# Dilated attention in a two-block fp32 program: operands split at the projection, a copy in eighths order, and softmax from head 0 up

## The chip, the cores and the metric

The program runs on one core of one Trainium2 chip. The metric is the device time of one execution in microseconds (us), the median of a few runs. Matrix products run on TensorE (PE in the rows, its weight loads PEld), elementwise work on VectorE (DVE) and ScalarE (ACT), a little on GpSimd (POOL), and SyncE (SP) issues nearly all DMAs.

## The reference

Two blocks follow each other on x of 1024 tokens by 1024 channels, in fp32. The first is a hybrid layer: an RMS norm, one projection, a gated delta rule ("GDN", 4 heads of 128), dilated attention (8 heads of 64), an output projection and a gated feed-forward. The second (spatial gating and a 31-tap convolution, then a feed-forward) is not touched by the diff. The part that matters:

```python
DIL_PATTERNS = ((128, 1), (512, 4), (2048, 16))
def dilated_attention(q, k, v):           # each (window, dilation): t, t-d, ..., t-window
    qf = q.transpose(0, 2, 1, 3) * (Dh ** -0.5)
    ...
    for window, dil in DIL_PATTERNS:
        num, den, m = band_attention(stride(qf), stride(kf), stride(vf), window // dil)
    ...
    m_all = jnp.maximum(jnp.maximum(ms[0], ms[1]), ms[2])
    wts = [jnp.exp(mi - m_all) for mi in ms]
    num_tot = wts[0] * nums[0] + wts[1] * nums[1] + wts[2] * nums[2]
    den_tot = wts[0] * dens[0] + wts[1] * dens[1] + wts[2] * dens[2]
    out = num_tot / den_tot
```

One maximum m_all per query over all three patterns is needed before the exponentials.

## The kernel before

**Precision.** A product of two fp32 operands is made of matmuls in a faster fp32 form (`fp32r`): each operand is split into a high part, rounded to that form, and a low part, the rest. For attention scores the splits are stacked over the partitions of one tile, so that two matmuls give a whole score block: one over 128 partitions (64 rows high part, 64 rows high or low part, tiles `KA`, `QA`) and one over 97 (64 rows, and rows 64 and 96, which add minus the maximum in the second pass; tiles `KB`, `QB`).

**Order.** The code is written as tasks (generators). A planner, run when the program is built, holds an assumed clock for each engine; `cost` adds the assumed time of each operation (`mm` for matmuls, `tp` for transposes, `act`, `tt`, `stt`, `dma`), and `run` always takes the task that, by these clocks and the tasks' priorities, can go next. What is emitted is a fixed order on every engine. Changing an assumed cost can so change the order anywhere. Tiles come from two arenas in SBUF, R (`arR`, fp32r operands) and F (`arF`, fp32); a task that asks for `room` waits until something is given back.

**The dilated part.** `proj1` computes queries and keys feature-major (`ps_dil`, 8 tiles of 128 rows by two halves of 512), ScalarE evacuates each, and they go to DRAM (`qd`, `kd`); values (`ps_dv`) follow. `dil` then makes two passes over the heads.

- The scan (`dil_scan`) takes a slot of 4 x 1024 words per head out of three, loads and splits keys and queries (`dil_split`: per operand two DMAs of 64x1024 into a staging tile, then ScalarE and VectorE), and computes 16 blocks of scores with *queries as the stationary operand* (`ps_S<-arR`, 32 matmuls a head). Eight blocks are 128 consecutive queries against their own and the previous block of keys ("pattern 0"). Eight are the queries r, r+8, r+16, ... ("eighths") against the 256 keys congruent to r modulo 4, which covers the other two patterns through a mask. VectorE adds the mask and takes each row's maximum in one operation (`djunk`, L1246). `dil_max` merges the maxima of four heads and writes them to DRAM (`mf`).
- The second pass (`dil_pv`) computes the scores again with *keys as the stationary operand* (`ps_T<-arR`, 32 matmuls a head), adds the mask on VectorE (tile `band`), takes the exponential on ScalarE, and multiplies by the values (`ps_O<-arF`, 48 matmuls a head). Heads come as 7, 6, 5, ..., 0; slots of heads 7 and 6 are kept from the scan, the others are loaded and split a second time (14 loads and splits in all are so made: 8 in the scan, 6 in the second pass). `dil_fin` divides and writes the operand of the output projection `ps_out`.

For the eighths blocks both operands are read with a step of 8 words (32 bytes): the stationary one is `slice(r, S, 8)`, the moving one comes from `eights`. The second pass waits for all maxima and for a reload of the mask (`band`), whose place was used by another half of it until the last maximum. When head 2 is done, its slot is given back and the weights of the output projection are fetched (`WH`, `weights(2)`).

The scan has the lowest priority of what PE can do at that time (7, against 2 for GDN), so that its matmuls fill the gaps in GDN's chains of small dependent matmuls (`ps_T<-arF`, `ps_pU`, `ps_G`, `ps_u`, `ps_o`).

Of the kernel before, what the change touches and what calls it, by code (L numbers as in the profile page):

```python
# [17 lines left out]
P = 128  # L18
# [73 lines left out]
class Weaver:  # L92
# [11 lines left out]
    STEP, SCP, KEEP1, KEEP0, WH = 2, 7, 2, 0, 2  # L104
# [154 lines left out]
class Prog(Weaver):  # L259
# [28 lines left out]
    def tp(self, out, in_):  # L288
        k = in_.shape[0]
        self.cost("PE", 107.0)  # L290
        self.nc.tensor.transpose(out, in_, self.ident[:k, :k])

    def tpacc(self, out, in_, start):

        self.cost("PE", 107.0)
# [307 lines left out]
    def proj1(self):  # L603
# [5 lines left out]
        self.qd, self.kd = d("qd", 512, S), d("kd", 512, S)  # L609
        self.ab = self.cp.tile([P, NT, 8], F32, name="ab")  # L610
        self.ssq = self.cp.tile([P, 8, NT], F32, name="ssq")
        raw, hl, st = self.fring(2, 2080), self.fring(3, 4160, "R"), self.fring(2, 520)
# [463 lines left out]
    def dil(self):  # L1076
# [5 lines left out]
        stg, heads = Ring([]), Ring([])  # L1082
        yield "SP", after(self.gmem)
        yield from self.more(stg, 2, S)
        mb = yield from self.room(2 * P)
        M = v3(mb.ap, P)
        scans, kept, maxs = [[], []], {}, [Ev(), Ev()]

        def head():
            b = yield from self.room(4 * S, arena=self.R)  # L1090
            heads.bufs.append(b)
            s = Slot(b.ap)
            s.buf = b
            self.spawn(self.dil_aug(s, heads), prio=4, eng="ACT")
# [12 lines left out]
        def scan():  # L1107
            for n, h in enumerate(range(8)):
                yield "SP", after(self.qkev[h // 4])
                s = yield from heads.get("SP")  # L1110
                keep = h in (7, 6)[:int(self.KEEP1)] or h in (3, 2)[:int(self.KEEP0)]
                if keep:
                    kept[h] = s
                scans[h // 4].append(self.spawn(self.dil_scan(h, s, None if keep else heads, stg, M), prio=int(self.SCP), eng="SP"))
# [6 lines left out]
            self.dma(self.band, self.a["c_band"][:, 768:1536], 393216)  # L1121
            self.turned.set(self.ready())

        self.turned = Ev()
# [31 lines left out]
        def allv():  # L1156
            yield "SP", after(self.vev)
            for pr in (3, 2, 1, 0):
                yield from loadv(pr)
# [3 lines left out]
        fins, last, loads = [], [], []  # L1163
# [952 lines left out]
```

## Time and profile before

| | us |
|---|---|
| median of 3 runs (lowest to highest) | 2617.27 (2617.18 to 2620.52) |
| the profiled execution's own time | 2619.11 |
| its span in the trace | 2617.3 |
| busy in the span: PE, DVE, ACT, POOL | 2540.3, 1370.7, 807.9, 121.1 |
| DMA bytes moved in the span | 170.80 MB |
| mean granted TensorE clock | 0.987 |

The profiled execution is 1.84 us above the median. PE has work for 97% of the span, so time is lost only in the gaps that its stages leave, or gained where its own instructions get shorter or fewer. The stages, on the span's time: projections to about 222 us, GDN with the dilated projections and the scan to about 636, the second pass to about 769, output projection and feed-forward to about 1600, and from there the second block to the end.

### The profile page before, as it was taken

The page shows a single profiled execution, that of the slowest core. Times are in us where ns is not written, and L with a number is a line of the kernel's source. Part 1 is how long each engine was busy: PE and PEld are TensorE (multiplying, and loading weights), DVE is VectorE, ACT ScalarE, POOL GpSimd, SP SyncE. Part 2 cuts the span into 40 slices and gives each one's busy share as a digit, 9 for nine tenths or more (in the row PEclk, how much of TensorE's full clock was granted, in tenths as well). Part 3 has the DMA queues.
Part 4 walks back from the last instruction along what each step waited for, and adds up shares of the span by engine and source line. Part 5 has one row for each costly group of instructions (what it writes and reads, how often), then busy time and mean ns, then how long its engine had stood idle before and what let it go on. Part 6 is the DMA issues. An engine that isn't in the chain of part 4 may idle for free.

```text
span 2617.3 us, 31361 instructions
## 1 busy us (share of the span) xinstructions
PE 2540.3 (97%) x13001; PEld 2180.4 (83%) x13001; DVE 1370.7 (52%) x1868; ACT 807.9 (31%) x1306; POOL 121.1 (5%) x245
## 2 busy tenths in 40 slices
PE   7999999988989999999999999989999999999998
PEld 6888999988978888888888888877788888888887
DVE  5441343454654555555555567969554444444444
ACT  5322443453541422222222235253232121212122
POOL 1010000000000000000000001050000000000000
PEclk9999999998989999999999999999999999999999
DMA  5232222232441111111111113102211111111111
GB/s 189 71 104 85 84 67 62 80 80 69 106 130 57 41 49 49 49 50 50 49 50 49 50 66 101 61 9 90 71 41 57 41 57 41 57 41 57 41 49 65
DMA packets 175164, 170.80 MB, mean 65 GB/s; under 512 B 25985, under 2 KB 148254, under 8 KB 175022
## 3 DMA queue, kind: packets, MB, share of 16 engines
q1 hardware_dynamic: 175022, 168.80, 21.2%
q8 instruction: 102, 1.67, 0.3%
q14 instruction: 40, 0.33, 0.0%
HBM read 145.50 MB, written 23.23 MB: 64 GB/s over the span
## 4 chain that ended last, share of the span: by engine, by line
PE 61%; issue 28%; DVE 4%; ACT 3%; DMA 2%; POOL 2%; SPq 0%; POOLq 0%; ACTq 0%; DVEq 0%
PE ps_up L281 18%; PE ps_dn L281 9%; PE ps_in L281 5%; PE ps_out L281 5%; PE ps_vg L281 3%; PE ps_dil L281 3%; PE ps_T L281 2%; ACT arF L311 2%; PE ps_S L281 2%; PE ps_z L281 2%; PE ps_O L281 2%; PE ps_dv L281 2%; DVE arF L327 2%; PE ps_pU L281 1%; PE ps_G L281 1%
## 5 line engine op out<-in xcount | busy, mean ns | idle before, releaser
L281 PE MATMUL ps_up<-arR 128*128 128x512 f32 x3648 | 831.5, 389 | 0.0
L281 PEld LDWEIGHTS ps_up<-arR 128*128 128x128 f32 x3648 | 684.5, 188 | 142.1
L315 DVE TENSOR_TENSOR arR<-arF,arR 128x1024 fp32r<-128x1024 f32 (+3 forms) x283 | 347.6, 1236 | 610.0 <-ACT arR L311 609.5
L281 PE MATMUL ps_dn<-arR 128*128 128x512 f32 x2592 | 591.8, 389 | 0.0
L311 ACT ACTIVATE arR<-arF 128x1024 fp32r<-128x1024 f32 (+3 forms) x297 | 311.2, 1071 | 852.3 <-PE ps_dn L281 394.3
L281 PEld LDWEIGHTS ps_dn<-arR 128*128 128x128 f32 x2592 | 486.4, 188 | 101.0
L315 DVE TENSOR_TENSOR arF<-arF,ps_dn 128x512 f32<-128x512 f32 x416 | 279.6, 684 | 183.2 <-PE ps_dn L281 183.2
L327 DVE SCALAR_TENSOR_TENSOR arF<-arF,pcol 128x1024 f32<-128x1024 f32 (+1 forms) x276 | 311.4, 1149 | 22.5 <-ACT arF L311 17.5
L311 ACT ACTIVATE arF<-arF 128x1024 f32<-128x1024 f32 (+3 forms) x158 | 134.8, 860 | 272.5 <-DVE arF L315 138.5
L281 PE MATMUL ps_out<-arR 128*128 128x512 f32 x768 | 182.2, 398 | 2.7 <-DVE arR L315 2.7
L281 PEld LDWEIGHTS ps_out<-arR 128*128 128x128 f32 x768 | 146.7, 192 | 34.4 <-DVE arR L315 3.7
L311 ACT ACTIVATE arF<-ps_up 128x512 f32<-128x512 f32 x152 | 89.5, 589 | 187.0 <-PE ps_up L281 187.0
L281 PE MATMUL ps_in<-arR 128*128 128x512 f32 x576 | 137.7, 399 | 0.0
L281 PEld LDWEIGHTS ps_in<-arR 128*128 128x128 f32 x576 | 109.4, 192 | 23.9
L315 DVE TENSOR_TENSOR arF<-arF 128x1024 f32<-128x1024 f32 (+4 forms) x91 | 89.1, 979 | 28.8 <-ACT arF L311 14.8
L281 PE MATMUL ps_dil<-arR 128*128 128x512 f32 x384 | 97.4, 403 | 0.0
L281 PE MATMUL ps_vg<-arR 128*128 128x512 f32 x384 | 88.3, 390 | 0.0
L281 PEld LDWEIGHTS ps_vg<-arR 128*128 128x128 f32 x384 | 71.8, 188 | 14.8
L281 PEld LDWEIGHTS ps_dil<-arR 128*128 128x128 f32 x384 | 71.7, 192 | 14.2
L281 PE MATMUL ps_O<-arF 128*128 128x128 f32 (+2 forms) x384 | 69.9, 328 | 12.2 <-ACT arF L311 6.8
L315 DVE TENSOR_TENSOR arF<-ps_G,csq 128x512 f32<-128x512 f32 x48 | 33.1, 690 | 90.8 <-PE ps_G L281 90.8
L315 DVE TENSOR_TENSOR arF<-arF,ps_out 128x512 f32<-128x512 f32 x64 | 43.5, 683 | 62.1 <-PE ps_out L281 62.1
(185 smaller groups left out, 2037.2 us busy)
## 6 DMA issues: line engine op xcount, KB each, us to landing
arF<-in_w_ff_dram SPq DMA_DIRECT2D x64, 512.0 KB
arF<-in_w_up_dram SPq DMA_DIRECT2D x44, 512.0 KB
arF<-in_w_in_dram SPq DMA_DIRECT2D x12, 1024.0 KB
arF<-in_w_down_dram SPq DMA_DIRECT2D x22, 512.0 KB
arF<-in_x_dram SPq DMA_DIRECT2D x16, 512.0 KB
arF<-in_w_out_dram SPq DMA_DIRECT2D x16, 512.0 KB
arF<-in_w_in_dram SPq DMA_DIRECT2D x16, 512.0 KB
arF<-kd SPq DMA_DIRECT2D x28, 256.0 KB
```

Of the source, the lines that this page charges most:

```text
L281: self.nc.tensor.matmul(out, lhsT, rhs, start=start, stop=stop, **kw)
L311: self.nc.scalar.activation(out, in_, func, **kw)
L315: self.nc.vector.tensor_tensor(out, a, b, op)
L327: self.nc.vector.scalar_tensor_tensor(out, a, s, b, op0, op1)
```

## The change

1. Queries and keys are split where they are evacuated from PSUM: ScalarE writes the high part, VectorE subtracts it from PSUM, and four tensors go to DRAM (`qh`, `ql`, `kh`, `kl`) with 32 stores of 256 KB in the place of 16. The staging slots there are twice as large.
2. `dil_split` and its staging ring are gone. `dil_fetch` brings three DMAs of 64x1024 words per operand, the stacked operand ready to use: six for each head in each pass. No slot is kept from the scan to the second pass, so 16 head loads (96 DMAs) are made where 14 (56 DMAs) were.
3. `dil_turn` makes a copy of the operand that is to be stationary, ordered by eighths (two ScalarE operations of 1024 columns a head and pass, which read with a step of 32 bytes). Stationary operands of eighths blocks are then consecutive columns. The moving operand is still read through `eights`.
4. The three slots of 4 x 1024 words become two `mov` slots (moving operand) and four `sta` slots (stationary operand, the eighths copy) of 2 x 1024 words. A head needs one `mov` and two `sta`, in either pass.
5. The mask of the second pass has a buffer of its own (`bb`, 768 words of F), loaded once at the start of `dil`.
6. The second pass takes heads 1, 0, 3, 2, 5, 4, 7, 6, each waiting for the maxima of its own group of four heads. `WH` is 7: weights are fetched from the last pair on.
7. The planner's assumed costs of matmuls and transposes change, with an assumed 240 ns for a matmul whose stationary operand is strided.

```diff
     def mm(self, out, lhsT, rhs, start, stop, loose=False):
         n, m = cols(rhs), cols(lhsT)
+        load = 112.0 if m > 64 else 56.0
         if rhs.dtype == F32:
-            c = max(1.667 * n, 213.0 if m > 64 else 107.0)
+            c = max(1.667 * n + 5.0, 2.0 * load)
         elif rhs.dtype == F32R:
-            c = max(0.417 * n, 107.0 if m > 64 else 56.0)
+            far = lhsT.ap[-1][0] > 1
+            c = max(0.417 * n + 13.3, 240.0 if far else load)
...
-                            self.act(s.ap[:, :H], ps, AF.Copy, scale=(0.125, 1.0)[part])
-                            self.dma((self.qd, self.kd)[part][m * P:(m + 1) * P, hf * H:(hf + 1) * H], s.ap[:, :H])
+                            hi, lo = (s.ap[:, x * H:(x + 1) * H].bitcast(F32R) for x in range(2))
+                            self.act(hi, ps, AF.Copy, scale=(0.125, 1.0)[part])
+                            if part:
+                                self.tt(lo, ps, hi.bitcast(F32), ALU.subtract)
+                            else:
+                                self.stt(lo, ps, 0.125, hi.bitcast(F32), ALU.mult, ALU.subtract)
+                            for x, dst in enumerate(self.qk[part]):
+                                self.dma(dst[m * P:(m + 1) * P, hf * H:(hf + 1) * H], s.ap[:, x * H:(x + 1) * H], 262144)
...
         mb = yield from self.room(2 * P)
         M = v3(mb.ap, P)
+        bb = yield from self.room(768)
+        self.dma(bb.ap, self.a["c_band"][:, 768:1536], 393216)
...
         def memory():
-            heads.bufs = []
-            yield from head()
+            yield from unit(mov)
+            yield from unit(sta)
             yield from self.opiece(1, 0)
-            for _ in range(2):
-                yield from head()
+            for r in (sta, mov, sta, sta):
+                yield from unit(r)
...
+        def load():
+            yield "SP", after(got)
+            for h in (1, 0, 3, 2, 5, 4, 7, 6):
+                box[h] = []
+                for r in (sta, sta, mov):
+                    box[h].append((yield from r.get("SP")))
+                kn, kr, q = box[h]
+                self.dil_fetch(1, h, kn)
+                e = self.spawn(self.dil_turn(kn, lambda kr=kr: kr), prio=4, eng="ACT")
+                self.dil_fetch(0, h, q)
+                self.spawn(self.dil_rows(h, q, after(e, maxs[h // 4]), here[h]), prio=4, eng="SP")
...
+    def dil_fetch(self, x, h, s):
         r = slice(h * 64, h * 64 + 64)
+        hi, lo = (d[r, :] for d in self.qk[x])
+        A, B = (s.ap[:, j * S:(j + 1) * S].bitcast(F32R) for j in range(2))
+        for o, i in ((A[0:64], hi), (A[64:128], (lo, hi)[x]), (B[0:64], (hi, lo)[x])):
+            self.dma(o, i, 262144)
+
+    def dil_turn(self, a, other):
+        yield "ACT", lambda: 0.0 if other() else -1.0
+        b = other()
+        turn = lambda t: t.rearrange("p (m r) -> p r m", r=8)
+        for o, n in ((0, P), (S, 64)):
+            self.act(v3(b.ap[:n, o:o + S], P), turn(a.ap[:n, o:o + S].bitcast(F32)))
...
+        yield "PE", after(turn)
+        self.put(sta, q)
+        q = other[0]
+        self.hold = True
         for g in range(4):
             yield "PE", after(*evs[-2:-1])
             ps = self.psum("S8")
             for x in range(2):
-                scores(ps[:, x * 256:x * 256 + 256], slice(g + 4 * x, S, 8), lambda t: self.eights(t, g))
+                r = g + 4 * x
+                scores(ps[:, x * 256:x * 256 + 256], q.ap, slice(r * P, (r + 1) * P), lambda t: self.eights(t, g))
```

What it moves, as the order of the built programs shows it. First PE in the midst of GDN, where the chain matmuls (`<-arF`) of one chunk stand between scan matmuls (`ps_S<-arR`) and projection matmuls (`ps_dil`). Before:

```order
L281 MATMUL ps_S<-arR 128x128 x2
L281 MATMUL ps_S<-arR 128x256 x2
L281 MATMUL ps_G<-arF 128x128 x4
L281 MATMUL ps_u<-arF 128x128 x8
L281 MATMUL ps_T<-arF 128x128 x4
L281 MATMUL ps_pU<-arF 128x128 x4
L281 MATMUL ps_S<-arF 128x128 x4
L281 MATMUL ps_o<-arF 128x128 x8
L281 MATMUL ps_G<-arF 128x128 x4
L281 MATMUL ps_S<-arR 128x256 x8
L281 MATMUL ps_dil<-arR 128x512 x6
```

The same place of the chunk's chain with the change:

```order
L283 MATMUL ps_dil<-arR 128x512 x24
L298 MATMUL ps_T<-csq,arF 128x128 x4
L283 MATMUL ps_dil<-arR 128x512 x6
L283 MATMUL ps_u<-arF 128x128 x8
L283 MATMUL ps_dil<-arR 128x512 x6
L283 MATMUL ps_S<-arF 128x128 x4
L283 MATMUL ps_o<-arF 128x128 x8
L298 MATMUL ps_pU<-csq,arF 128x128 x4
L283 MATMUL ps_G<-arF 128x128 x4
L283 MATMUL ps_dil<-arR 128x512 x6
L283 MATMUL ps_T<-arF 128x128 x4
L283 MATMUL ps_pU<-arF 128x128 x4
```

There is no scan matmul left here: only `ps_dil` (and later `ps_dv`) stands between the chains. The second place is PE at the end of GDN. Before, with the last chains:

```order
L281 MATMUL ps_S<-arR 128x256 x8
L281 MATMUL ps_G<-arF 128x128 x4
L281 MATMUL ps_S_4714<-arR 128x256 x4
L281 MATMUL ps_T<-arF 128x128 x4
L281 MATMUL ps_pU<-arF 128x128 x4
L291 MATMUL ps_ot<-csq,arF 128x128 x4
L281 MATMUL ps_S_4744<-arR 128x256 x4
L281 MATMUL ps_S_4749<-arR 128x256 x4
L281 MATMUL ps_G<-arF 128x128 x4
L281 MATMUL ps_S_4764<-arR 128x256 x4
L281 MATMUL ps_pU<-arF 128x128 x4
L291 MATMUL ps_mt<-csq,mt 16x128
```

With the change, the same chains and what follows them:

```order
L283 MATMUL ps_T<-arF 128x128 x4
L283 MATMUL ps_pU<-arF 128x128 x4
L283 MATMUL ps_G<-arF 128x128 x4
L293 MATMUL ps_ot<-csq,arF 128x128 x4
L283 MATMUL ps_T<-arF 128x128 x4
L283 MATMUL ps_pU<-arF 128x128 x4
L283 MATMUL ps_G<-arF 128x128 x4
L283 MATMUL ps_pU<-arF 128x128 x4
L283 MATMUL ps_S_4275<-arR 128x256 x4
L283 MATMUL ps_S_4282<-arR 128x256 x4
L283 MATMUL ps_S<-arR 128x128 x2
L283 MATMUL ps_S<-arR 128x256 x2
```

The chains stand alone, and the scan begins behind them: apart from 16 matmuls of head 0, which stand earlier, 240 of its 256 matmuls come in one piece here, with only the last `ps_w`, `ps_u`, `ps_o` and `ps_ot` of GDN among them. The third place is SP at the start of the second pass (`vd` are values, `mf` maxima, `kd` and `qd` the operands). Before:

```order
L339 DMA arF<-zd 128x512
L339 DMA arF<-vd 128x8x64 x4
L339 DMA arR<-mf_102 1x1024
L339 DMA arR<-mf_103 1x1024
L339 DMA arR<-mf_102 1x1024
L339 DMA arR<-mf_103 1x1024
L339 DMA arF<-kd 64x1024 x4
L339 DMA band<-in_c_band_dram 128x768
L339 DMA arF<-in_x_dram 128x1024 x2
L339 DMA arF<-qd 64x1024 x2
```

With the change (`md` are the row maxima of one head on their way to the merge):

```order
L341 DMA arR<-kh 64x1024 x2
L341 DMA arR<-kl 64x1024
L341 DMA arR<-qh 64x1024
L341 DMA arR<-ql 64x1024
L341 DMA arR<-qh 64x1024
L341 DMA arF<-md 8x128
L341 DMA arF<-md 8x8x16
L341 DMA md<-mtt 16x128
L341 DMA arR<-mf_104 1x1024
L341 DMA arR<-mf_105 1x1024
```

The first heads' operands are asked for ahead of the last maxima, values have been loaded well before, the mask's load is gone from here, and a head has six loads of 64x1024 in the place of four.

## Rows read from the trace of the kernel before

**Rows 1.** The page, part 1: busy time of each engine.

```profile
PE 2540.3 (97%) x13001; PEld 2180.4 (83%) x13001; DVE 1370.7 (52%) x1868; ACT 807.9 (31%) x1306; POOL 121.1 (5%) x245
```

**Rows 2.** Windows by stage: length, then busy us of each engine (instructions), clock, DMA.

```profile
core 0: us, PE busy (x) PEld busy (x) DVE busy (x) ACT busy (x) POOL busy (x), PEclk, DMA share, GB/s
222.00:636.00 414.00, 395.90 (x2869) 374.10 (x2867) 172.72 (x489) 179.21 (x358) 13.30 (x25) 0.99 0.24 70
636.00:650.00 14.00, 6.13 (x28) 5.29 (x28) 5.39 (x11) 2.59 (x5) 1.41 (x3) 0.76 1.06 266
650.00:769.00 119.00, 109.28 (x617) 104.13 (x618) 74.15 (x110) 66.13 (x97) 2.10 (x4) 0.94 0.46 117
769.00:800.00 31.00, 28.99 (x112) 23.23 (x112) 15.62 (x19) 4.99 (x5) 0.00 (x0) 0.88 0.39 119
1600.00:1860.00 260.00, 244.31 (x1316) 208.40 (x1316) 213.97 (x237) 98.57 (x235) 41.84 (x49) 0.97 0.20 63
```

**Rows 3.** The chain of waits around the start of the second pass: start, us.

```profile
637.88 4.56 DMA arF<-vd
643.12 5.33 DMA band<-in_c_band_dram
650.04 2.05 PE ps_O L281 x8
```

**Rows 4.** Timeline of PE in the second pass, runs of like matmuls: start, us.

```profile
660.09 1.30 PE L281 MATMUL ps_T<-arR 128*128 128x256 f32 x4
661.22 1.04 PE L281 MATMUL ps_O<-arF 128*128 128x256 f32 x4
661.91 2.27 PE L281 MATMUL ps_T<-arR 128*128 128x256 f32 x8
664.00 2.25 PE L281 MATMUL ps_O<-arF 128*128 128x256 f32 x11
```

**Rows 5.** Groups by form, 222 to 800 us: count, busy us, mean ns, idle before.

```profile
L281 PE MATMUL ps_dv<-arR 128*128 128x256 f32 x384 | 49.1, 283 | 0.0
L1246 DVE CUSTOM_DVE_ANT_0 djunk<-ps_S,band 128x256 f32<-128x256 f32 x120 | 45.4, 419 | 17.7 <-PE ps_S L281 17.0
L315 DVE TENSOR_TENSOR arR<-arF,arR 64x1024 fp32r<-64x1024 f32 x28 | 34.1, 1217 | 26.1 <-ACT arR L311 25.7
L311 ACT ACTIVATE arR<-arF 64x1024 fp32r<-64x1024 f32 x14 | 14.6, 1044 | 0.0
L315 DVE TENSOR_TENSOR arF<-ps_T,band 128x512 f32<-128x512 f32 x56 | 37.2, 687 | 22.3 <-PE ps_T L281 20.0 <-ACT arF L311 1.3 <-DMA band<-in_c_band_dram 0.9
```

**Rows 6.** Timeline of DVE in the scan, two row maxima in close order.

```profile
588.83 0.42 DVE L1246 CUSTOM_DVE_ANT_0 djunk<-ps_S,band 128x256 f32<-128x256 f32 x1
589.18 0.42 DVE L1246 CUSTOM_DVE_ANT_0 djunk<-ps_S,band 128x256 f32<-128x256 f32 x1
```

**Rows 7.** Timeline of SP: one issue of four loads of 64x1024.

```profile
640.68 2.40 SPq L339 DMA_DIRECT2D arF<-kd  x4
```

**Rows 8.** DMA view, 640 to 656 us, 40 slices of 0.4 us.

```profile
GB/s 229 216 218 191 104 164 287 287 318 215 266 215 246 236 241 233 202 200 366 397 461 369 440 369 461 389 317 246 215 236 174 21 10 20 0 0 0 0 0 0
```

**Rows 9.** Timeline of ACT: 512 columns read in order, and with a step (`dil_fin`).

```profile
649.27 1.83 ACT L311 ACTIVATE arF<-arF 128x512 f32<-128x512 f32 x3 [2.86 <-DVE arF L315]
697.74 2.08 ACT L311 ACTIVATE arR<-arF 128x512 fp32r<-128x512 f32 x2
```

**Rows 10.** The chain of waits inside the second pass: start, us.

```profile
716.23 3.78 DMA rd<-den
721.81 5.72 DMA arF<-qd
727.61 2.00 ACT arR L311 x2
```

**Rows 11.** PE's waits, 1600 to 1860 us: total, times, longest.

```profile
PE ps_ct L281 <- DVE arF L327: 7.8, 2, 5.6
PE ps_c L281 <- ACT arF L311: 6.4, 1, 6.4
```

More of the change, by code (lines that the diff above doesn't have):

```diff
@@ L103 @@
     ISSUE, N1P, SSL, CLL = 475.0, 2, 6000.0, 1500.0
[L104 removed]
+    STEP, SCP, WH = 2, 7, 7
     KP0, KP1, KP2, KP3 = 0, 0, 0, 3
@@ L1109, in scan @@
                 yield "SP", after(self.qkev[h // 4])
[L1110 to L1114, printed above, removed]
+                k = yield from mov.get("SP")
+                q = yield from sta.get("SP")
+                scans[h // 4].append(self.spawn(self.dil_scan(h, k, q, mov, sta, M, got if h == 7 else None), prio=int(self.SCP), eng="SP"))
                 if n % 4 == 3:
@@ L1157, in allv @@
             yield "SP", after(self.vev)
-            for pr in (3, 2, 1, 0):
+            for pr in range(4):
                 yield from loadv(pr)
@@ L1162, in dil @@
         self.spawn(allv(), prio=6, eng="SP")
-        fins, last, loads = [], [], []
-        for pr in (3, 2, 1, 0):
+        box, here = {}, [Ev() for _ in range(8)]
+        def load():
[10 more added lines that the diff above has]
+                self.hold = True
+                yield "SP"
+        self.spawn(load(), prio=4, eng="SP")
+        fins, last = [], []
+        for pr in range(4):
             den, ob = [], {}
@@ L1167, in dil @@
                 h = 2 * pr + hh
-                yield "SP", after(*maxs, self.vev)
-                box = [kept.get(h)]
-                e = self.spawn(self.dil_load(h, box, heads, stg), prio=3, eng="SP")
-                loads.append(e)
-                last = [self.spawn(self.dil_pv(pr, hh, box, e, V, vr, ptr, stage, ob, heads), prio=5, eng="PE")]
+                yield "SP", after(self.vev)
+                last = [self.spawn(self.dil_pv(pr, hh, box, here[h], bb.ap, V, vr, ptr, stage, ob, mov, sta), prio=5, eng="PE")]
                 den += last
@@ L1176, in dil @@
             fins.append(self.spawn(self.dil_fin(pr, ob, den, stage, recr), prio=4, eng="SP"))
-        yield "SP", after(*loads)
-        yield from self.drain(stg, 2)
         yield "SP", after(*last)
-        for r, n in ((heads, 2), (ptr, int(self.PTR))):
+        bb.give()
+        for r, n in ((sta, 2), (mov, 1), (ptr, int(self.PTR))):
             yield from self.drain(r, n)
@@ new lines, in dil_rows, with dil_scan, room @@
+    def dil_rows(self, h, q, cond, done):
+        yield "SP", cond
+        for r, d in zip((64, 96), self.mf):
+            self.dma(q.ap[r:r + 1, S:2 * S].bitcast(F32), d[h:h + 1, :])
+        done.set(self.ready())
+    def dil_scan(self, h, k, q, mov, sta, M, got):
+        nc = self.nc
+        self.dil_fetch(0, h, q)
+        self.dil_fetch(1, h, k)
+        landed = self.ready()
+        KA, KB = (k.ap[:, j * S:(j + 1) * S] for j in range(2))
+        other = []
+        def room():
+            other.append((yield from sta.get("ACT")))
+            if got:
+                got.set(self.ready())
+        turn = self.spawn(self.dil_turn(q, lambda: other and other[0]), prio=4, eng="ACT", t=landed)
+        self.spawn(room(), prio=4, eng="ACT", t=0.0)
@@ L1269, in dil_scan @@
                 self.hold = True
-        if heads is not None:
-            self.put(heads, s)
+        self.put(sta, q)
+        self.put(mov, k)
         yield "PE", after(*evs)
@@ L1312, in dil_max, with dil_pv, back @@
         done.set(self.ready())
-    def dil_load(self, h, box, heads, stg):
-        if not box[0]:
-            yield from self.dil_split(h, box, stg, heads)
-        QB = box[0].ap[:, 3 * S:]
-        for r, d in zip((64, 96), self.mf):
-            self.dma(QB[r:r + 1].bitcast(F32), d[h:h + 1, :])
-    def dil_pv(self, pr, hh, box, e, V, vr, ptr, stage, ob, heads):
-        h = 2 * pr + hh
-        yield "PE", after(e, self.turned)
-        hs = box[0]
-        KA, KB, QA, QB = (hs.ap[:, j * S:(j + 1) * S] for j in range(4))
+    def dil_pv(self, pr, hh, box, e, mk, V, vr, ptr, stage, ob, mov, sta):
+        h = 2 * pr + hh
+        yield "PE", after(e)
+        kn, kr, q = box.pop(h)
+        QA, QB = (q.ap[:, j * S:(j + 1) * S] for j in range(2))
+        def back(ring, s):
+            if h == int(self.WH):
+                s.buf.give()
+            else:
+                self.put(ring, s)
         loaded = lambda pat: lambda: V[pr, pat][2].t if (pr, pat) in V else -1.0
```

93 lines of the change are left out of this document (34 added, 59 removed).

## The prediction, on record before the change was run

> **What bounds the kernel now.** I read the busy times first: PE works for 97% of the span and DVE for 52% [rows 1]. So the time is PE's own work plus its gaps, and the windows by stage say where the gaps are [rows 2]. From 222 to 636 us (GDN, dilated projections, scan) PE is busy for 395.9 of 414 us: 18 us of gaps. From 636 to 650 it is busy for 6.1 of 14 us, at a granted clock of 0.76, while the DMA share is 1.06. The second pass, 650 to 769, holds 109.3 us of PE work in 119 us. Then 2 of 31 us are idle, and in the start of the second block (1600 to 1860) 15.7 of 260. DVE and ACT are far from full in all of these but the last, where DVE has 214 of 260 us.
>
> The chain of waits explains the gap at 636: values are loaded until 642.4, then the mask of the second pass from 643.1 to 648.5, and only at 650.0 does the first product with values start [rows 3]. That is a start-up stall of about 14 us with 6 us of work in it.
>
> The price of a strided stationary operand comes from PE's timeline [rows 4]. Four eighths matmuls take 661.22 - 660.09 = 1.13 us, eight take 664.00 - 661.91 = 2.09 us. The difference is 0.24 us a matmul, and each run pays about 0.17 us more at its ends. The 256-column matmuls of the value projection, both operands in order, are 384 in 49.1 us, 0.128 us each [rows 5]. So 128 eighths matmuls of the second pass carry up to 128 x (0.24 - 0.128) = 14.3 us that the stride costs, and as much again in the scan.
>
> **The change, part by part.** *Split at the projection.* 16 more DVE operations of 128x512 out of PSUM, about 0.69 us each by the mask addition of that shape [rows 5], are 11 us. They fall between 222 and 440, within the stretch where DVE is busy for 173 of 414 us [rows 2]. Cost 0 while `ps_dil` is filler; if each held a PSUM buffer for its 0.69 us in PE's way, 11 us. I take 0. The 16 more stores (16 x 0.6 us of SP, by the issue rate in [rows 7]) lie in the same stretch, where nothing is queued behind them that PE soon needs.
>
> *Splits removed.* 28 DVE operations of 1.22 us (34 us) go [rows 5], with the ScalarE operations ahead of them. They are off the path except where a head's load is late in the second pass: `qd` lands after 5.72 us and two ScalarE operations take 2.00 us more [rows 10]. In their place a head has six loads (1.57 MB) for four.
>
> *The copy by eighths.* The trace has no matmul with a stationary operand in order and a moving one with a step. Lower bound 0.128 us, as both in order; upper bound 0.24, as both strided, for then the change of the weights' order buys nothing. A weight load has 128 columns and the moving pass 256, so both may be near 0.24 or only the load. I take 0.20, nearer to the strided row, since the moving operand keeps its stride. That saves 0.04 us a matmul and most of the 0.17 us at a run's ends. Per head of the second pass PE now has 109.3 / 8 = 13.7 us; with four runs a head, it loses 16 x 0.04 + 4 x 0.17 = 1.3 us and has about 12.3 us. The copy costs ScalarE two operations of 1024 columns: 1.04 us each if the step costs nothing [rows 5], and 2 x 1.04 us each by the stepped read of 512 columns, which takes 1.04 us where 512 in order take 0.61 [rows 9]. I take the upper end, 4.1 us a head, as that read too has a step. ScalarE has 66 of 119 us in the second pass; 8 x 4.1 = 33 us more, less 6 heads' splits, leave it under 90.
>
> *The scan moved behind GDN.* The order shows it: with the change nothing but `ps_dil` and `ps_dv` fills GDN's gaps, its last chains stand alone, and 240 of the 256 scan matmuls come after. Scan work inside 222 to 636 was 128 x 0.128 + 128 x 0.24 + 32 x 0.17 for the runs' ends = 52 us; 2 us of it (16 matmuls) stay ahead. So without the scan the stretch has 395.9 - 52 + 2 = 346 us of PE work, of which about 5 us (`ps_w`, `ps_u`, `ps_o`) stand inside the later scan: 341. Its 18 us of gaps do not all go, since the last chains have no filler: I keep 14. It then ends at 222 + 341 + 14 = 577 us.
>
> The scan alone, per head: PE 16 x 0.128 + 16 x 0.20 = 5.3 us; DVE 16 maxima at a start-to-start of 0.35 us [rows 6] = 5.5 us; SP six issues at 0.60 us [rows 7] and three small ones, about 4.5 us; 1.57 MB at the 250 GB/s that the view shows while many loads are under way [rows 8], 6.3 us; ScalarE's copy up to 4.1 us. No resource needs more than 6.3 us, but a head holds one of two `mov` slots from its first load to its last matmul: 3.6 us of issues, some 5 us until the last has landed, half the copy (2 us) beyond pattern 0's 2.7 us, then 2.6 us: 14 us, for two heads at a time 7 us each. Two heads are loaded ahead: 2 x 5.5 + 5.5 x 7 = 50 us. Lower bound 7.5 x 5.5 = 41 us (DVE alone), upper bound below. The second pass then begins at 627, its first value product at about 629, where it was 650.0.
>
> *The second pass.* 8 x 12.3 = 98 us of PE work, plus the 9.7 us of gaps that the old one has within 119, is 108 us. What is late next there is the slot again: two heads may be under way, and the third one's six loads start when the first gives its slots back, then the copy (up to 4.1 us) and the two rows of maxima, some 14 us for the 12.3 us that the head between needs. That would add up to 2 us a head; against it, the loads no longer wait for splits. I keep the 9.7 us and let the range go 12 us up. The pass ends at 737, where it was 769: 32 us earlier. Start-up stall, shorter matmuls and the copies' cost are all within this number.
>
> *After it.* Weights of the output projection are asked for about one head before the end, where they had more than two heads; the gap of 2 us there may grow by 2. The planner's new costs also reorder the dense parts and the second block, whose gaps come to 14.2 us in two groups [rows 11]. Nothing in the trace says which way; I take 0 and put 6 us on either side into the range.
>
> **The sum.** 2619.1 (the profiled execution, 1.8 above the median) - 32 + 2 = 2589; against the median, **2587 us**.
>
> **Rivals.** *A, the scan alone is bound by its slots* (slower). If loads, copy and matmuls of the two heads do not overlap (both share one SP queue, and a load of 5.7 us after its issue is seen in [rows 10]), a head takes its 14 us plus waits behind the other's issues, about 16 us for each. Then 2 x 5.5 + 5.5 x 16 = 99 us for 50: 2587 + 49 = 2636. It decides from 50 + 30 = 80 us on, 12.5 us a head, where the gain is gone. For it speaks that the scan before was spread over 400 us and never had to run at this rate; against it that no queue or engine has more than 6.3 us to do a head. 0.18, of which 0.12 ends above and 0.06 within the bound of no change.
>
> *B, the copy buys nothing*, since the moving operand with its step is as slow as the strided weights. Then the second pass has 8 x 16 x 0.04 = 5 us more and the scan up to 2: 2587 + 7 = 2594. For it speaks that a strided run never goes below 0.24 us in the trace, against it that the loads there show no room beside them. [...] 0.20.
>
> *C, the moving operand's step is free* and the scan goes at DVE's pace. Eighths matmuls take 0.128 us, so the second pass loses 8 x 16 x 0.072 = 9 us more, and the scan 9: 2587 - 18 = 2569. 0.12.
>
> My forecast itself has 0.50, with a range of its own of 2576 to 2599.
>
> **How the numbers follow.** A measurement of this kernel can tell about 0.2%, 5 us, from no change. Forecast, B and C are faster: 0.50 + 0.20 + 0.12 = 0.82. A gives 0.06 for the same and 0.12 for slower. The range goes down to 2562 (C with 6 us more from the dense parts and 1 from the stall) and up to 2611, where A has not yet eaten the gain; what lies outside is about 0.12 of A above it and a few hundredths of C below.
>
> **What would show each step.** In the changed profile, `ps_S<-arR` should be almost absent before about 575 us, and the stretch from there to the first `ps_T<-arR` should take 45 to 60 us. Start-to-start of eighths matmuls should be near 0.20 us (0.24 is B, 0.13 is C). The waits of `ps_S` in the scan should name ScalarE's copy or a load; 12 us or more a head is A. ScalarE's operations of 1024 columns with `arR` on both sides should last about 2 us. The first `ps_O` should come near 629, right behind the first `ps_T`, without a wait on a mask, and the last some 108 us later. The stretch from the first `ps_out` to the end should be within 6 us of what it was. The prediction is wrong if the tail of GDN without filler has far more than 14 us of gaps, if the scan waits for slots, or if the second pass waits for its loads at each head.

## The result and the profile after

The changed kernel takes 2637.51 us (median of 4, 2636.86 to 2638.93) against 2617.22 us: a ratio of 1.0079, 95% interval 1.0062 to 1.0096. It is 20 us slower, where 30 us less was forecast. Numbers below that are read from a trace belong to one profiled execution, which took 2637.78 us.

First the windows of the changed kernel, cut at its own stages; columns as in [rows 2].

```profile
core 0: us, PE busy (x) PEld busy (x) DVE busy (x) ACT busy (x) POOL busy (x), PEclk, DMA share, GB/s
222.00:571.00 349.00, 335.91 (x2556) 316.80 (x2555) 121.29 (x245) 151.85 (x320) 11.99 (x23) 0.99 0.26 80
571.00:648.00 77.00, 59.41 (x300) 54.03 (x298) 47.59 (x249) 40.01 (x31) 2.45 (x5) 0.78 0.77 177
650.00:778.00 128.00, 109.68 (x632) 100.72 (x632) 62.81 (x102) 78.01 (x96) 2.11 (x4) 0.89 0.62 149
778.00:868.00 90.00, 90.00 (x415) 75.06 (x414) 44.39 (x59) 21.04 (x30) 4.46 (x12) 1.00 0.23 71
1595.00:1824.00 229.00, 208.84 (x1127) 178.82 (x1125) 183.93 (x198) 95.50 (x207) 42.93 (x55) 0.96 0.18 58
```

The scan does stand alone, from 571 to 648: 59 us of PE work in 77 us, at a mean granted clock of 0.78. From its first product on, the second pass takes 128 us where it took 119, with 62.8 us of DVE where it had 74.2, and 78.0 us of ACT where it had 66.1 [rows 2]. The first product with values comes 2 us behind the first `ps_T`, where a stall of 10 us was [rows 3], but no earlier than before. Laid side by side, by the first or last matmul of each kind in the timelines (the last two columns are experiments below):

| us | before | changed | e3, old costs | e5, old costs in the second block |
|---|---|---|---|---|
| first `ps_dil` | 223.1 | 219.5 | 222.4 | 220.6 |
| first `ps_T` of the second pass | 640.0 | 647.9 | 635.6 | 648.4 |
| first product with values | 650.0 | 650.2 | 645.5 | 650.6 |
| end of the second pass | 768.9 | 777.9 | 770.2 | 780.3 |
| first matmul of the second block | 1590.3 | 1595.4 | 1585.8 | 1595.9 |
| its first `ps_out` | 1797.8 | 1824.5 | 1793.5 | 1803.6 |
| end of that `ps_out` | 1909.5 | 1928.4 | 1904.5 | 1914.2 |
| last matmul | 2609.4 | 2628.3 | 2604.3 | 2614.1 |

Of the 19 us that the last matmul comes later, 14 arise in the second block, where the diff changes no operation: 319.2 us from its first matmul to the end of its `ps_out` are now 333.0. The other 5 stand before it. PE is busy for 307.8 of the 333.0 us, at a granted clock of 0.96 up to the first `ps_out` and 0.97 behind it; before it was busy for 303.5 of 319.2, at 0.98 and 0.97. So the gaps grow from 15.7 to 25.2 us, and the busy time by 4.3. What PE waits for there (changed kernel, 1580 to 1930 us; total, times, longest):

```profile
PE ps_cb L293 <- ACT arF L313: 9.9, 3, 6.9
PE ps_ct L283 <- DVE arF L329: 9.8, 2, 5.0
PE ps_vg L283 <- DVE arR L317: 3.3, 2, 3.1
PE ps_u L283 <- DVE arR L317: 2.2, 2, 1.4
```

The waits on `ps_cb` answer to those on `ps_c` before [rows 11], and are 3.5 us longer; those on `ps_ct` are 2 us longer; those on `ps_vg` and `ps_u` come to 5.5 us, where the kernel before has 0.4. The longest stands in the timeline of PE, with its idle time in brackets: between `ps_ct` and `ps_cb`, which waits for what ScalarE makes of it, there are only 48 matmuls of 0.12 us.

```profile
1712.72 1.06 PE L283 MATMUL ps_ct<-csq,arF 128*128 128x128 f32 x8
1713.54 5.99 PE L283 MATMUL ps_v<-arR 128*128 128x256 f32 x48
1726.38 1.25 PE L293 MATMUL ps_cb<-csq,arF 128*128 128x128 f32 x4 [6.85 <-ACT arF L313]
```

Before, all 24 `ps_ct` stood in one group behind 312 `ps_v`, and what waits for ScalarE came once:

```profile
1721.10 2.84 PE L281 MATMUL ps_ct<-csq,arF 128*128 128x128 f32 x24
1730.29 5.37 PE L281 MATMUL ps_c<-arF 128*128 128x512 f32 x6 [6.35 <-ACT arF L311]
```

The price of an eighths matmul, in the timeline of PE in the second pass: a run of four in-order blocks, then a run of four eighths.

```profile
666.96 0.66 PE L283 MATMUL ps_T<-arR 128*128 128x256 f32 x4
667.46 1.12 PE L283 MATMUL ps_O<-arF 128*128 128x128 f32 x8
668.33 1.12 PE L283 MATMUL ps_T<-arR 128*128 128x256 f32 x4
669.27 1.09 PE L283 MATMUL ps_O<-arF 128*128 128x128 f32 x8
```

In order, four take 667.46 - 666.96 = 0.50 us, but the last two of these have only 128 columns each (the last block of pattern 0); full blocks in order start 0.12 us apart at full clock, here as before. Eighths, now with their stationary operand in order, take 0.94 us, where both operands in steps took 1.13 [rows 4]. The single starts in this run lie 0.217 to 0.220 us apart, after 0.27 for the first, where they were 0.240 to 0.247 apart after 0.40. A weight load falls from about 340 to 206 ns, and what stays above 0.12 us stays with the step of the moving operand, in which alone these matmuls differ from those in order. So 32 runs save, by estimate, 32 x 0.19 = 6 us a pass.

The copies, by form (busy us, mean ns, idle before):

```profile
L313 ACT ACTIVATE arR<-arR 128x1024 fp32r<-128x1024 f32 x16 | 33.5, 2092 | 8.1 <-DMA arR<-ql 6.1 <-DMA arR<-kh 1.8
L313 ACT ACTIVATE arR<-arR 64x1024 fp32r<-64x1024 f32 x16 | 33.3, 2082 | 0.0
```

In the second pass 4 us of them stand ahead of exponentials in ScalarE's queue. Timelines of ACT (two copies, then three exponentials) and of PE:

```profile
698.67 3.99 ACT L313 ACTIVATE arR<-arR 128x1024 fp32r<-128x1024 f32 x2
702.56 1.55 ACT L313 ACTIVATE arF<-arF 128x512 f32<-128x512 f32 x3
```

```profile
703.23 1.01 PE L283 MATMUL ps_O<-arF 128*128 128x128 f32 x3 [4.84 <-ACT arF L313]
```

Over the pass PE waits 18.2 us for exponentials, in 9 waits, where before it waited 6.8 us, in 4.

In the scan, the chain of waits (start, us) goes through each head's last load and through the round trip of the row maxima:

```profile
591.06 6.75 DMA arR<-kl
606.22 4.82 DMA md<-mtt
622.45 6.08 DMA arR<-kl
632.82 6.76 DMA arR<-kl
641.22 6.20 DMA md<-mtt
```

SP itself waits there for the maxima's store before it reads them back, and the next heads' loads stand behind it in its queue (waits of SP, 571 to 648):

```profile
SPq L341 <- DMA md<-mtt: 19.2, 5, 5.7
SPq L341 <- PE ps_S L283: 10.9, 8, 5.5
```

### The profile page after: what moved, and what is told of

Same layout as the page of the kernel before. It is cut to its first block, busy times and chain, and to the rows that moved or that the text cites. A ratio compares the mean times of both kernels' runs of the same rounds, so it can differ in the third digit from the quotient of the medians.

```text
span 2636.0 us, 31486 instructions
## 1 busy us (share of the span) xinstructions
PE 2539.9 (96%) x13001; PEld 2174.5 (82%) x13001; DVE 1351.7 (51%) x1856; ACT 841.2 (32%) x1304; POOL 123.9 (5%) x245
## 4 chain that ended last, share of the span: by engine, by line
PE 59%; issue 28%; ACT 4%; DVE 4%; DMA 2%; POOL 2%; SPq 0%; POOLq 0%; ACTq 0%; DVEq 0%
PE ps_up L283 18%; PE ps_dn L283 8%; PE ps_out L283 6%; PE ps_in L283 5%; PE ps_dil L283 3%; PE ps_vg L283 3%; PE ps_T L283 2%; ACT arF L313 2%; ACT arR L313 2%; PE ps_z L283 2%; PE ps_dv L283 2%; PE ps_pU L283 2%; PE ps_G L283 1%; PE ps_S L283 1%; DVE arF L329 1%
## 5 line engine op out<-in xcount | busy, mean ns | idle before, releaser
L283 PE MATMUL ps_up<-arR 128*128 128x512 f32 x3648 | 831.5, 389 | 0.0
L317 DVE TENSOR_TENSOR arR<-arF,arR 128x1024 fp32r<-128x1024 f32 (+2 forms) x255 | 313.8, 1239 | 585.0 <-ACT arR L313 584.9
L313 ACT ACTIVATE arR<-arF 128x1024 fp32r<-128x1024 f32 (+2 forms) x255 | 268.7, 1076 | 845.4 <-PE ps_dn L283 394.2
L313 ACT ACTIVATE arF<-arF 128x1024 f32<-128x1024 f32 (+2 forms) x158 | 134.6, 859 | 294.8 <-DVE arF L317 139.1
L283 PE MATMUL ps_O<-arF 128*128 128x128 f32 (+2 forms) x384 | 74.4, 339 | 18.3 <-ACT arF L313 18.2
L283 PEld LDWEIGHTS ps_O<-arF 128*128 128x128 f32 x384 | 62.7, 212 | 25.2 <-ACT arF L313 21.8
```

The lines of the kernel that those rows point to most:

```text
L283: self.nc.tensor.matmul(out, lhsT, rhs, start=start, stop=stop, **kw)
L313: self.nc.scalar.activation(out, in_, func, **kw)
L317: self.nc.vector.tensor_tensor(out, a, b, op)
```

## The experiments

Theory 1: the scan is dear because it stands alone. Theory 2: the new table of assumed costs gives a worse order. Theory 3: the copies on ScalarE cost more than they bring.

**e1_units_first.** `dil` asks for the mask's buffer before its slots. In the planner's run another task (`opiece(0, 0)`) takes the free piece of R in that moment, and the first slot comes some 200 us later by the planner's clock (on the chip, the first head's loads are issued near 470 us, and near 298 in this run).

```diff
-        bb = yield from self.room(768)
-        self.dma(bb.ap, ...)
...
         self.spawn(memory(), prio=4, eng="SP")
+        self.spawn(mask(), prio=4, eng="SP")    # room(768) and its load
```

> The changed kernel with one order of requests turned round: the slots of R are asked for before the mask's buffer of its own, which a task of its own then takes. Theory 1 (the scan stands alone because the slots come 200 us late, and then runs with gaps and at half the clock, 76 us): about half of the scan goes back among GDN's chains and the value projection, the second pass starts 15 to 25 us earlier, 2610 to 2622 us. Theory 2 (the planner's new cost table): no change, 2632 to 2643. Theory 3 (the copies on ScalarE slow both passes): as in the changed kernel, 2630 to 2640.

Measured: 2631.19 us (1.0052, 1.0037 to 1.0067). The scan starts at 313 us where it started at 480, and the second pass ends at 771.7: 6 us gained, not 15 to 25. A part of theory 1 at most: the time lies in the range of theory 3.

**e2_units_first_scan_strided.** As e1, and:

```diff
-        yield "PE", after(turn)
-        self.put(sta, q)
-        q = other[0]
...
-    scores(ps[...], q.ap, slice(r * P, (r + 1) * P), lambda t: self.eights(t, g))
+    scores(ps[...], q.ap, slice(r, S, 8), lambda t: self.eights(t, g))
```

> As e1_units_first, and the scan makes no copy by eighths: its stationary queries are read with their step, as before, so a head holds one mov and one sta slot. Theory 1: the whole scan is filler again and the second pass starts near 600 us; with the second pass still 127 us long, 2590 to 2605 us. Theory 2: 2630 or more. Theory 3: the scan's 33 us of copies go, but those of the second pass stay, 2615 to 2630.

Measured: 2637.23 us (1.0078, 1.0061 to 1.0095). The scan is filler (its last matmul at 563 us) and the second pass begins at 608.6, as expected, yet it ends at 774.1. The value projection now lasts until 587.6 and GDN's last `ps_o` until 669.4, where the changed kernel had 547.7 and 584.0. What was taken out of the scan's place came back as GDN chains beside the second pass. The total is the changed kernel's. Theory 1 falls as the main cause: where the scan stands moves the waits, not their sum.

**e3_old_costs.** The changed kernel without the `mm` and `tp` lines of the diff (its first hunk taken back).

> The changed kernel with the old table of assumed costs in the planner. Theory 1: the scan still stands alone, so the 21 us lost at the start of the second pass stay; only the second block, whose gaps grew from 15.7 to 26.8 us, may come back: 2624 to 2634. Theory 2 (the table moves the scan too): 2617 or less. Theory 3: 2632 to 2640.

Measured: 2615.07 us (0.9993, 0.9983 to 1.0002), 22 us less than the changed kernel, in the range of theory 2. Windows of it, second block up to its `ps_out`: its gaps are back to 8 us in 207.

```profile
1586.00:1793.00 207.00, 199.24 (x1099) 171.06 (x1098) 167.21 (x183) 80.88 (x175) 40.14 (x51) 0.98 0.17 52
```

Its second pass starts with a stall again: the first product comes 9.9 us behind the first `ps_T`, with one long wait for the rows of maxima in between. The changed kernel has no such wait; its scan ends 12 us later.

```profile
PE ps_T L281 <- DMA arR<-mf: 7.0, 1, 7.0
```

**e4_new_costs_alone.** The kernel before with that hunk alone.

> The kernel before with only the new table of assumed costs. Theory 1: the scan stays filler, and only the second block's gaps may grow as in the changed kernel: 2615 to 2629. Theory 2 (the table is the cause): 2630 or more. Theory 3: 2617 with 4 us on either side.

Measured: 2631.67 us (1.0056, 1.0041 to 1.0071). The table alone costs the kernel before 14 us, all of it in the second block, which takes 333.0 us for 319.2; ahead of that block this run is 3 us earlier than before. The time is just beyond the 2630 from which it speaks for theory 2.

**e5_old_costs_second_block.** The changed kernel; behind `c = ...` the old costs hold once the planner's PE clock has passed 1450 us, so that only the second block is in its old order (the same holds for transposes).

```diff
+        if self.free["PE"] > 1450000.0 and rhs.dtype in (F32, F32R):
+            c = ...    # as in the kernel before
         self.cost("PE", c)
```

> The changed kernel, with the old table of assumed costs only from the feed-forward's later part on, so that the second block stands in the order of before and all ahead of it in the changed one. Theory 2a (the new table's order of the second block costs 14 us, and the dilated part's own loss is only about 6): 2621 to 2626 us. Rival (what e3_old_costs gave back came from the dilated part's order): 2632 or more.

Measured: 2623.62 us (1.0024, 1.0013 to 1.0036). So of the 22 us between the changed kernel and e3, 13.9 are the second block's order and 8.5 the order ahead of it, as theory 2a had it. Of the latter, in the profiled executions, about half stands ahead of the first product (650.6 us, in e3 645.5) and half in the pass (129.7 us, in e3 124.7).

**e12_one_entry_of_the_table.** The kernel before with

```diff
-            c = max(0.417 * n, 107.0 if m > 64 else 56.0)
+            c = max(0.417 * n + 13.3, 112.0 if m > 64 else 56.0)
```

> The kernel before with one entry of the cost table changed: an fp32r matmul is assumed to take 0.417 ns a column plus 13.3 ns (227 ns for 512 columns, where the trace has 228) in the place of 0.417 ns a column alone (213 ns). If this entry alone gives the second block its slower order: 2628 to 2634, as e4_new_costs_alone. If it needs the other entries: 2614 to 2621.

Measured: 2631.41 us (1.0059, 1.0044 to 1.0074). This entry does it alone: the second block takes 334.1 us, and the waits in its first part are much like those of the changed kernel:

```profile
PE ps_cb L291 <- ACT arF L311: 9.7, 3, 6.9
PE ps_ct L281 <- DVE arF L327: 6.9, 1, 6.9
```

The entry is nearer to the trace: 512 columns are now assumed at 227 ns, and 3648 `ps_up` matmuls keep PE busy for 831.5 us, 228 ns each. A truer cost gave a worse order.

**e6_copy_on_gpsimd.** As e3, and `dil_turn` of the second pass on GpSimd:

```diff
+                self.nc.gpsimd.tensor_copy(v3(b.ap[:n, o:o + S], P), turn(a.ap[:n, o:o + S].bitcast(F32)))
```

> As e3_old_costs (2615 us), and in the second pass the copy by eighths is made on GpSimd, which is idle there, in the place of ScalarE. Theory 3 for the second pass alone (two copies of 2.09 us a head stand ahead of exponentials in ScalarE's queue, and PE waits 15.6 us for them): those waits fall to about 7 us as before the change, and the pass gets 8 to 14 us shorter, 2601 to 2608. Rival a (the pass is bound by its loads): 2612 to 2618. Rival b (the copy on GpSimd takes so long that the scores wait for it): 2620 or more.

Measured: 2612.97 us (0.9986, 0.9977 to 0.9996). 2 us better than e3, not 8: PE still waits 14.7 us for exponentials. The time is in the range of rival a, but PE has no long wait for loads inside the pass. The timeline of POOL and DVE shows a new delay in front of the longest wait for exponentials (4.9 us), the split in `dil_fin` at twice its time beside the copy (two of these operations took 2.08 us in the changed kernel, at 697.31):

```profile
686.91 4.77 POOL L1238 CAST arR<-arR 128x1024 fp32r<-128x1024 f32 x2 [9.28 <-DMA arR<-kh]
688.37 4.13 DVE L315 TENSOR_TENSOR arR<-arF,arR 128x512 fp32r<-128x512 f32 x2 [1.73 <-ACT arR L311]
```

Another pair of these operations took 3.36 us (at 724.30, in the chain of waits). The rest of DVE's work, most of it the mask additions, whose one operand lies in PSUM, took no longer beside the copies: DVE is busy for 67.5 us in the pass where it has 64.2 in e3, with 103 operations in both, and the two pairs take 3.3 us more than 2.08 us each. What holds up the other 10 us of exponentials stays open.

**e7_no_copy_second_pass.** As e3, the second pass takes no third slot and reads `kn.ap, slice(r, S, 8)`.

> As e3_old_costs (2615 us), and the second pass makes no copy: its stationary keys of the eighths are read with their step. PE's work grows by 128 x 0.12 = 15 us, ScalarE has 33 us less. If the copies cost the pass as much as they bring: 2611 to 2619. If their delay of the exponentials is the larger (theory 3): below 2611. If the shorter matmuls are worth their copies: above 2619.

Measured: 2615.30 us (0.9994, 0.9984 to 1.0003), as e3. The pass itself is 115.1 us from first to last product where e3 has 124.7, so the copies cost it 10 us more than they bring; PE's waits for exponentials are 6.9 us. (With both operands in steps an eighths matmul took 0.240 us in the kernel before, for 0.218 in the changed one, so PE's work grows, by estimate, by the 6 us a pass from above, not by the 15 of the expectation. PE's busy time does not show it, 111.2 us in the pass for 112.0 in e3, at a granted clock of 0.93 for 0.87.) But the output projection behind it then takes 97.5 us, where it had 90.4: with the pass over sooner, it waits for the last heads' operand (`ps_out <- DVE arR`, 3.6 us) at a granted clock of 0.96.

**e8_scan_filler_copy_on_gpsimd.** e6 and e2 together.

> As e6_copy_on_gpsimd, with the slots asked for first and a scan without copies as in e2_units_first_scan_strided. Theory 1 (a scan that is filler again is worth what it loses standing alone): 8 us or more below e6_copy_on_gpsimd. Rival, after e2: what the scan gains as filler is lost again, since GDN's last chains then stand beside the second pass; within 5 us of e6_copy_on_gpsimd or above it.

Measured: 2625.44 us (1.0033, 1.0020 to 1.0046), 12 us above e6: the rival. PE waits 21.6 us in the second pass for the rows of maxima.

**e9_lookahead_5.** As e3, with `LA` 5 in the place of 3.

> As e3_old_costs (2615 us), with five score tiles computed ahead of the product with values in the second pass in the place of three. If PE's waits for the exponentials there (15.6 us, behind ScalarE's copies) are a matter of too little work ahead: they fall below 8 us, the granted clock in the pass rises above 0.90 and the pass gets 8 to 15 us shorter, 2600 to 2608. If ScalarE and VectorE cannot go faster through the pass, or the last heads' division sets its end: 2612 to 2618.

Measured: 2615.20 us (0.9992, 0.9982 to 1.0001). The waits for exponentials fall to 7.8 us and the pass takes 111.2 us from first to last product, as the first theory had it, but the output projection takes 103.2: it waits 6.1 us for ScalarE's and 3.4 us for VectorE's part of the last operand. The total is the rival's.

**e10_no_copy_lookahead_5.** e7 and e9 together.

> As e7_no_copy_second_pass (2615 us), with five tiles ahead. PE waits only 6.9 us for exponentials there, so the same reasoning gives 3 to 6 us less at most: 2609 to 2615.

Measured: 2608.57 us (0.9968, 0.9957 to 0.9979), faster than both kernels and just below the expectation. Windows of the pass: PE is busy for 102.7 of 105 us at full clock, with both operands of the eighths in steps.

```profile
649.00:754.00 105.00, 102.71 (x620) 99.17 (x620) 57.97 (x94) 47.70 (x76) 2.10 (x4) 1.00 0.66 162
```

**e13_before_lookahead_5.** The kernel before with `LA` 5.

> The kernel before with five score tiles ahead in the second pass in the place of three, nothing else. If the 9 us that e10_no_copy_lookahead_5 gained over the kernel before come from the lookahead: 2606 to 2612. If they need the split at the projection and the new order of heads: 2614 to 2620.

Measured: 2610.78 us (0.9972, 0.9962 to 0.9982). So what e10 gains is the lookahead; the split, the new order of heads and the two slot sizes are worth about 2 us beside it, no more than can be told. Here too the output projection ends what can be gained (waits of PE, 640 to 860):

```profile
PE ps_out L281 <- ACT arR L311: 6.7, 1, 6.7
PE ps_out L281 <- DVE arR L315: 3.4, 1, 3.4
PE ps_O L281 <- ACT arF L311: 3.2, 1, 3.2
```

**e11_fill_scan_gaps.** The changed kernel, in its own order, with matmuls whose results nothing reads:

```diff
+            if not g and h:
+                for _ in range(32):
+                    nc.tensor.matmul(ps[:, 0:P], self.maskb, self.identb, start=True, stop=True, ...)
```

> The changed kernel (2637.5 us) in its own order, with 32 small bf16 matmuls, whose results are overwritten, ahead of each of the two patterns of heads 1 to 7 in the scan. They are 448 matmuls more, about 25 us of PE's time if nothing hid them. If the scan's matmuls are slow because the gaps let the granted clock fall to half: the clock of 571 to 648 us rises from about 0.8 to above 0.9, the scan's matmuls come every 0.12 us, and the stretch stays within 5 us of its 76 us or gets shorter: 2630 to 2642. If the clock is not the reason: it gets 10 to 25 us longer, 2647 to 2662.

Measured: 2643.71 us (1.0103, 1.0088 to 1.0118), 6 us above the changed kernel, between the two expectations. Windows of the scan, then its timeline:

```profile
571.00:654.00 83.00, 77.61 (x753) 71.71 (x752) 47.67 (x250) 42.11 (x32) 2.45 (x5) 0.98 0.71 165
```

```profile
630.32 3.71 PE L283 MATMUL ps_S<-arR 128*128 128x256 f32 x16
633.85 1.98 PE L1283 MATMUL ps_S<-identb,maskb 128*128 128x128 bf16 x32
```

The mean granted clock is 0.98 where it was 0.78. The 32 fillers of this timeline end where the next run starts, at 635.64, so one takes 0.056 us, and of 448 x 0.056 = 25 us of fillers only 6 show: the rest lay in gaps. But the stretch did not get shorter for it. A head's 16 eighths still take 633.85 - 630.32 = 3.53 us, 0.22 each, with the scan's mean clock at 0.98. So their price is the step of the moving operand, not the clock. The changed kernel's own trace says the same: from 598.5 to 604.0 us, after a wait of 4.62 us for a load, the granted clock is 0.50; in-order matmuls of 256 columns start 0.213 us apart there, for 0.120 at 1.00, but eighths 0.217 there, for 0.218.

**e14_no_copies_at_all.** e10, and the scan without copies; three `mov` and three `sta` slots.

> As e10_no_copy_lookahead_5 (2609 us), without the copy in the scan either, and with the R memory that this frees as a third slot for moving operands (three and three). Theory: the copy in the scan costs more than it brings, since it holds a second slot and ScalarE, and saves 7 us of PE; heads go round faster with three slots: 2597 to 2606. Rival: the scan and the end of the second pass are set elsewhere (loads at 230 GB/s, the last heads' division): 2606 to 2613. If the copy in the scan pays: above 2613.

Measured: 2617.60 us (0.9999, 0.9989 to 1.0008), 9 us above e10. By the expectation the scan's copy pays, but the trace speaks of something else too: PE waits 11.8 us for the rows of maxima at the start of the pass, where e10 waits 7.1 there. How much of the 9 us is the copy's stays open, since the slots and SP's order changed with it; a scan copy alone, with all else kept, was not tried.

**e15_rows_from_gpsimd.** e14, the two loads of a head's rows moved to GpSimd's queue:

```diff
-            self.dma(q.ap[r:r + 1, S:2 * S].bitcast(F32), d[h:h + 1, :])
+            self.nc.gpsimd.dma_start(q.ap[r:r + 1, S:2 * S].bitcast(F32), d[h:h + 1, :])
```

> As e14_no_copies_at_all, with the loads of the two rows of maxima issued by GpSimd in the place of SP. If PE's wait of about 7 us for these rows at the start of the second pass is their place in SP's queue, behind the round trips of later heads' maxima: the wait falls below 3 us, 3 to 6 us less than e14_no_copies_at_all. If it is the transfer itself: the same within 3 us.

Measured: 2619.90 us (1.0014, 1.0004 to 1.0024). The wait for the rows is gone, and a wait of 7.4 us for the first exponentials stands in its place. The time is within the 3 us of the second expectation, but neither account holds: the wait moved, with nothing gained.

## Why the prediction was wrong

The forecast missed by 50 us. On the span's time, the second pass ends at 777.9 where 737 was forecast: the scan begins 6 us sooner, but lasts 27 us longer, and the pass lasts 20 us longer. Behind it 2 us were added and 9.9 measured: 14 us more in the second block, 2 in the feed-forward, and 6 less in the output projection. Three steps failed.

**The step that makes the kernel slower than before** is the one on the planner: "Nothing in the trace says which way; I take 0 and put 6 us on either side into the range". It cost 13.9 us in the second block (e5), which one entry of the table does alone in the kernel before (e12), and 8.5 us ahead of it. That the diff touches no operation there was no ground for so small a bound: the block's gaps of 14.2 us [rows 11] could have warned, and the order with the change could be read before any run. The kernel before has one group of 24 `ps_ct` there and one long wait behind it; the new order has groups of 8 and of 16 among the `ps_v`, and PE waits behind either (6.85 us, then 2.0 and 1.1). I took "reordered" as a symmetrical unknown; that an order with few gaps has more ways to get worse is my reading, from this one case.

**The second pass**, 108 us forecast, 127.7 measured. PE saves 6 us, not 10.4: 0.20 us was taken for an eighths matmul and 0.218 measured, and a run's ends gave 0.10 us of the 0.17 that I took. The copy's own price was right, 4.2 us for 4.1. What failed is "leave it under 90": I summed ScalarE's work and did not ask what stands behind the copy in its queue. The exponentials do, PE waits 18.2 us for them, and the granted clock is 0.89. e7 shows it, with the old table, by taking the copies away: 115.1 us for 124.7.

**The scan alone**: it began at 571 (577 forecast), and lasted 77 us for 50. A head's round trip was costed at 14 us, two heads at a time; the chain shows 6.1 to 6.8 us for the last load, where I had 5, and 4.8 to 6.2 us for the store of the maxima to DRAM, of which I had counted only the issue. That SP's queue holds the next head's loads behind this trip (19.2 us of SP's waits) is what was missed. This is read from the trace: no run took the trip out of SP's queue in the scan, so how much of the 27 us it explains stays open. The lower clock cost, by estimate, about 6 us of it: 59.4 us of PE work at 0.78, against 77.6 - 25 = 53 at 0.98 in e11. e1 and e2 show that putting the scan back among GDN's chains gains at most 6 us.

**Right**: GDN's tail without the scan left 13 us of gaps (14 forecast), the splits at the projection cost nothing (0.96 of the stretch 222 to 571 is PE work, and none of its long waits is on `ps_dil`), and no gain shows from the splits that DVE no longer makes (e10 against e13). The wait for the mask at the start of the pass is gone, and in the changed kernel the whole stall with it (2.3 us from the first `ps_T` to the first product, for 10); in e3 a wait for the rows of maxima takes its place.

**Between the forecast and its rivals**: the moving operand's step stayed dear. 0.218 us for an eighths matmul lies between my 0.20 and the 0.24 of rival B, and the 6 us that PE saves in a pass are near B's sum (10.4 - 5). An eighths matmul took 0.240 us with both operands at a step of 32 bytes and takes 0.218 with only the moving one so, where a block with both in order takes 0.12: most of the price stayed, as B had it. Rival A named 2636 us, but that it came so near is luck: it asked for a scan of 99 us, and the scan took 77, 9.6 us a head where 12 were to be its sign.

**Where the gain went**: with the old table (e3) the change is worth 2 us, which the measurement cannot tell from nothing. There the first product with values comes 4.5 us earlier than before, the pass takes 124.7 us for 118.9, and the output projection 90.4 for 96.3. In the pass PE's 6 us were saved, and more came back as waits for ScalarE (15.6 us for 6.8); at its start the wait for the mask became one of 7.0 us for the rows. When the waits for ScalarE are removed (e7, e9, e10), the output projection waits for the last heads' operand, up to 9.5 us. Open is what the scan's copy is worth by itself (e14), and why the order ahead of the second block loses 8.5 us with the new table, which in the kernel before loses nothing there (e4): e1 gains 6.3 in that stretch by the order of two requests, and whether these are part of the 8.5 was not tried.

## What to carry to other kernels

A table of assumed costs is part of every stage that a planner orders: change it alone first, and compare the order in the stages that should not move. A saving on the busiest engine is worth what its partners leave of it: before an operation is put on an idle engine, look at what is queued behind it there. Where two operands are strided, putting one in order may leave most of the price with the other (0.240 us became 0.218, where both in order take 0.12).

## What the runs showed of the hardware

- Both operands with a step of 32 bytes: 0.240 us from start to start for an fp32r matmul of 256 columns at a granted clock of 1.00 (the kernel before); only the moving one: 0.218 (the changed kernel); none: 0.12 (both). Between the two kernels a weight load of the eighths falls from 340 to 206 ns when its operand is put in order and the moving one keeps its step.
- With a stepped moving operand the clock does not show: 0.217 us at a granted clock of 0.50, 0.218 at 1.00, in the changed kernel's scan. In order it is 0.213 and 0.120.
- A ScalarE copy of 1024 columns with a step of 32 bytes takes 2.09 us on 128 partitions and 2.08 us on 64 (the changed kernel); on GpSimd 2.09 and 2.16 us (e6).
- Beside such a copy on GpSimd, two VectorE subtractions of 128x512 with both operands in SBUF took 4.13 us, without it 2.08 (e6 and the changed kernel). The rest of DVE's work in the pass, mask additions with one operand in PSUM among it, took no longer than in e3, which has no copies on GpSimd (67.5 us for 64.2, with 3.3 in two pairs of such subtractions).
